# First layer of a two-layer hybrid mixer: norm scratch of the routings on other bytes, rotation and gate tables loaded with the mixer pools

## Chip, core and metric

The kernel runs on one core of a Trainium2 chip. Time is the device time of one execution in microseconds; three runs of the kernel before gave a median of 4283.43 us (4277.82 to 4283.72). TensorE is called PE here, VectorE DVE, ScalarE ACT, GpSimd POOL and SyncE SP; SP issues the plain loads, POOL the indirect ones.

## The reference, cut to what matters

Two layers work on 512 latent tokens x (four tiles of 128) and 256 context tokens (two tiles), 1024 wide. Each layer has a mixer of three parallel parts and then PEER, a retrieval from 16384 single-neuron experts. The context is needed through the first layer only. The function is this, with the arguments cut:

```python
for l in range(DEPTH):                       # 2
    hx = rmsnorm(x, norm1_g[l]) * (1.0 + sc1) + sh1
    hc = rmsnorm(ctx, norm1_g[l]) * (1.0 + csc1) + csh1
    yx, yc = token_mixer(hx, hc, ...)        # one input projection w_in; RG-LRU, latent attention, Hyena; w_out
    x = x + g1 * yx
    hx = rmsnorm(x, norm2_g[l]) * (1.0 + sc2) + sh2
    x = x + g2 * peer(hx, ...)
    if l < DEPTH - 1:                        # the same for ctx
        ctx = ctx + cg1 * yc ...; ctx = ctx + cg2 * peer(hc, ...)
return rmsnorm(x, final_g)

def block(xb):                               # peer, for 128 tokens
    q = (xb @ wq).reshape(T, 8, 256)         # 8 heads, two half queries against 128 keys each
    v1, i1 = lax.top_k(s1, 16); v2, i2 = lax.top_k(s2, 16)
    top_s, top_p = lax.top_k(cand, 16)       # 16 of the 256 sums
    eid, gate = ..., softmax(top_s)          # 128 experts for a token
    act = gelu(einsum('td,thkd->thk', xb, u_tab[eid]))
    return einsum('thk,thkd->td', gate * act, v_tab[eid])
```

## The kernel before

The program (`schedule`) writes down the first layer in this order: the context's mixer, with the Hyena filters and the modulation; the context's `route` (selection of experts, both tiles of kind "G"); x's mixer (`front`, `back`); the context's expert work; x's route and experts (`peer_x`); then the second layer. Experts are computed in one of two ways. For tiles of kind "D" (three of x's four in the first layer) `peer_x` multiplies with all experts: `ublock` makes 128 blocks of products (pst), `weights` builds the gates as one-hot products (og, o1, o2, pwt), `vblock` adds up the output (dacc). For tiles of kind "G" the rows of the chosen experts are gathered one row for each token at a time (`rows_of`, an indirect DMA on POOL into one of five buffers `grow`); DVE then does one step for each: `gtile_u` a product with a sum (acc and dot, L1100), `gtile_v` a weighted addition (acc, L1113). The context's two tiles and x's fourth are of kind G: 2 x 128 steps for each, 768 in the first layer.

Each piece of the program has a priority (`prio`): 1 for the context's mixer and its route, 3 for x, 6 for the gathers. A scheduler that builds the kernel sets each engine's order from the priorities and from its own estimate of when operands and bytes are ready; on the chip, each engine works its list in order. Tiles live in pools on a left and a right stack of on-chip memory; a tile of a later pool that lies on bytes of an earlier one has to wait until the last reader of the earlier one is done.

The steps that matter: `front` makes x's first norm (`transposed`: xr, xn, the transposes ptr, hT), loads w_in in 18 blocks (L522), multiplies (pwin, 16 matmul records for each block, 288 in all) and convolves (hc, xx, L545 and L547); then come the RG-LRU with its gate table gw (L704, read by L714) and Hyena (first spectral product ht, L651). `back` makes the latent attention `mla`, which loads the rotation tables ropep, ropec and ropes (L785 to L789; first read at L768), then the output projection pwo in four tiles, each followed by two DVE operations (wotmp, xs at L589 and L595), a store, and the second norm of that tile, which is the first step of x's `route`. `route` takes A2 and B2 (rows of the modulation), norms and transposes the tiles (into dhT for kind D, rhT for others), gives the norm's scratch back, and only then opens the pool rt with the keys, the weights wpq and the selections (top16: MAX8 at L981 and so on; experts: eid at L1060; gates). For the context both pools lie on the right stack at the same place, one after the other; for x the norm's scratch (`rn`) lies above what `back` has given back.

Of the kernel before, what the change touches and what calls it, by code (L numbers as in the profile page):

```python
# [71 lines left out]
class Kern:  # L72
# [50 lines left out]
    def run(self):  # L123
        tc, nc, a = self.tc, self.nc, self.a
        with ExitStack() as es:
# [16 lines left out]
            self.iota = pp.tile([128, 128], F32, name="iota")  # L142
            nc.gpsimd.iota(self.iota, pattern=[[1, 128]], base=0, channel_multiplier=0,
                           allow_small_or_imprecise_dtypes=True)
            self.iotah = pp.tile([128, 128], F16, name="iotah")
            nc.vector.tensor_copy(self.iotah, self.iota)
            self.ranks = pp.tile([128, 16, 8], F16, name="ranks")
            nc.vector.tensor_copy(self.ranks, self.iota[:, 0:16].unsqueeze(2).to_broadcast([128, 16, 8]))
# [24 lines left out]
    def schedule(self):  # L173
        a = self.a
        with ExitStack() as er:
# [31 lines left out]
            with self.prio(3):  # L207
                gx, ex = self.peer_x(0, 384, 6, 32, 32, (36, 46, 46), ex)
# [12 lines left out]
            with self.prio(5):  # L221
                gx, _ = self.peer_x(1, 320, 0, 32, 46, (44, 42, 42), ex)
# [231 lines left out]
    def front(self, es, ps, pr, l, s, low, side="left", split=True, ctx=False):  # L454
# [7 lines left out]
        st["cat"] = mp.tile([128, KD, L], F32, name="cat")  # L462
        st["cq"] = [mp.tile([128, L], F32, name=f"cq_{i}") for i in range(3)]
# [5 lines left out]
        st["u1"] = [lp.tile([128, L], F32, name=f"u1_{i}") for i in range(3)]  # L469
        sc = None  # L470
# [78 lines left out]
    def back(self, ps, pr, l, s, st, ex, mods=()):  # L549
# [6 lines left out]
        with self.pool(f"wo{l}{s}", side="right") as sp, ExitStack() as es2:  # L556
# [17 lines left out]
            tp = es2.enter_context(self.pool(f"wot{l}{s}", side=st["side"]))  # L574
            load(tp, later)
            g = self.load_row(tp, l, 0, s, "g1")
            for t in range(nt):
# [10 lines left out]
                tmp = tp.tile([128, D], F32, name="wotmp", bufs=2)  # L588
# [4 lines left out]
                else:  # L593
                    old = self.res[s][:, t, :]
                nc.vector.tensor_add(self.res[s][:, t, :], old, tmp)  # L595
                nc.sync.dma_start(self.sd[s][t], self.res[s][:, t, :])
                self.dump(f"xm{l}{s}{t}", self.res[s][:, t, :])
        self.src[s] = [self.sd[s][t] for t in range(nt)]

# [98 lines left out]
    def lru(self, ps, l, s, st, full, mp):  # L698
# [3 lines left out]
        with self.pool(f"lru{l}{s}", side="right") as sp:  # L702
            gw = sp.tile([128, 2, 2, 3, 128], F32, name="gw")
            nc.sync.dma_start(gw, a["lru_g"][l])  # L704
# [57 lines left out]

    def rope(self, sp, ps, t, rope):
# [10 lines left out]
    def mla(self, ps, pr, l, s, st, full, mods=iter(()), pool=None):  # L774
# [4 lines left out]
        with nullcontext(pool) if pool else self.pool(f"mla{l}{s}", side=st["side"]) as sp:  # L779
# [3 lines left out]
            if not s:  # L783
                pm = sp.tile([96, 96], F32, name="ropep")
                nc.sync.dma_start(pm, a["ropep"])  # L785
                cst = sp.tile([128, 512], F32, name="ropec")
                nc.sync.dma_start(cst[64:96, :], a["ropec"])
                snt = sp.tile([128, 512], F32, name="ropes")
                nc.sync.dma_start(snt[64:96, :], a["ropes"])  # L789
                rope = (pm, cst, snt)  # L790
# [99 lines left out]
    def route(self, ps, l, s, kinds, hT=None, iT=None, i2n=None, side="left", done=None, fill=iter(())):  # L890
# [8 lines left out]
        with ExitStack() as es:  # L899
            if hT is None:  # L900
# [16 lines left out]
            if done:  # L917
                done.close()
# [512 lines left out]
```

## Time and profile before

| | |
|---|---|
| median of 3 runs | 4283.43 us (4277.82 to 4283.72) |
| profiled execution | 4280.5 us |
| its span | 4278.7 us |
| mean granted clock of PE | 0.937 |
| PE busy | 3732.9 us, 87% |
| DVE busy | 3506.5 us, 82% |
| ACT, POOL busy | 44%, 36% |
| gathers' DMA queue | 604.05 MB, 40.6% of the 16 engines' span |
| chain that ended last | PE 33%, DMA 21%, DVE 17%, issue 16%, POOL 7% |

Busy time is an average over stages with different limits. In time the program runs like this: the context's mixer to about 371 us, the context's route to 538, x's projections to 609.5, Hyena and RG-LRU to about 690, latent attention to 829, output projection to 881, x's second norm and route to 1244, the dense experts to 2474, and the second layer from there to 4278.7. The chain of waits names, at each step, what released the next one; "issue" in it is time in which nothing that the profile shows was waited for.

### The profile page before, as it was taken

To read this page: it belongs to the slowest core of one execution; us is meant where nothing else is said; L and a number is where in the kernel's file an instruction comes from. 1 tells how busy PE (TensorE), PEld (TensorE's weight loads), DVE (VectorE), ACT (ScalarE), POOL (GpSimd) and SP (SyncE) were. 2 spreads that over 40 slices of the span, in tenths; PEclk is the share of its full clock that TensorE was granted. 3 is DMA by queue.
4 is the path that set the end of the run, shared out by engine and by line. 5 is a ranking of instruction groups with operands and counts; after the bars stand their busy time and mean duration, and the time that the engine had idled before them with its cause. 6 is when DMAs were issued, how large, how long until landed. Compare 5 with 4: busy or idle time off the path is not lost.

```text
span 4278.7 us, 63806 instructions
## 1 busy us (share of the span) xinstructions
PE 3732.9 (87%) x22530; PEld 2815.8 (66%) x22530; DVE 3506.5 (82%) x7435; ACT 1898.1 (44%) x3715; POOL 1524.6 (36%) x1225
## 2 busy tenths in 40 slices
PE   7887987968989989998868979887889999999997
PEld 3645544548878877877656657446888887776654
DVE  5746987889989988988898874754899998888988
ACT  4454342533247525622462233633325655555732
POOL 0000244652344563366426620000126345553243
PEclk7998997988999999999989989998999999999998
DMA  5554587885768897799879962252359888887697
GB/s 195 199 199 153 202 310 233 280 300 195 243 223 270 309 353 258 236 364 357 287 228 330 353 205 90 70 157 95 117 194 336 284 295 304 291 293 279 225 353 273
DMA packets 305154, 1062.90 MB, mean 248 GB/s; under 512 B 35468, under 2 KB 42336, under 8 KB 304834
## 3 DMA queue, kind: packets, MB, share of 16 engines
q0 software_dynamic: 165888, 604.05, 40.6%
q1 hardware_dynamic: 138946, 454.78, 30.5%
q8 instruction: 177, 2.90, 0.3%
q14 instruction: 143, 1.17, 0.1%
HBM read 1041.85 MB, written 16.84 MB: 247 GB/s over the span
## 4 chain that ended last, share of the span: by engine, by line
PE 33%; DMA 21%; DVE 17%; issue 16%; POOL 7%; ACT 5%; SPq 0%; POOLq 0%; DVEq 0%; ACTq 0%
PE pst L121 7%; POOL grow L1089 7%; DMA grow<-in_peer_u_dram,eid 6%; PE dacc L121 6%; DMA grow<-in_peer_v_dram,eid 5%; PE pwin L121 4%; DMA uv<-in_peer_ut_dram 4%; DMA uv<-in_peer_v_dram 4%; DVE uvl L114 3%; PE ppq L121 3%; DVE acc L1100 2%; DVE acc L1113 2%; DMA wmod<-in_w_mod_dram 2%; PE pwo L121 2%; PE fp L404 1%
## 5 line engine op out<-in xcount | busy, mean ns | idle before, releaser
L1089 POOL DMA_INDIRECT grow<-in_peer_u_dram,eid x576 | 754.0, 1309 | 1144.2 <-DVE acc L1100 562.0
L1089 POOL DMA_INDIRECT grow<-in_peer_v_dram,eid x576 | 762.7, 1324 | 767.3 <-DVE acc L1113 623.8
L121 PE MATMUL pst<-dhT,uvh 128*128 128x384 f32 (+1 forms) x4096 | 997.9, 328 | 0.0
L113 ACT CAST uvh<-uv 128x1024 fp32r<-128x1024 f32 x491 | 513.0, 1045 | 689.6 <-DMA uv<-in_peer_v_dram 414.2
L121 PE MATMUL pst<-dhT,uvl 128*128 128x384 f32 (+1 forms) x2048 | 695.1, 340 | 106.6 <-DVE uvl L114 75.0
L1113 DVE SCALAR_TENSOR_TENSOR acc<-grow,gate,acc 128x1024 f32<-128x1024 f32 x571 | 732.9, 1284 | 52.1 <-DMA grow<-in_peer_v_dram,eid 45.2
L1100 DVE SCALAR_TENSOR_TENSOR acc<-grow,ghx 128x1024 f32<-128x1024 f32 x576 | 704.6, 1223 | 66.7 <-DMA grow<-in_peer_u_dram,eid 61.3
L114 DVE TENSOR_TENSOR uvl<-uv,uvh 128x1024 fp32r<-128x1024 f32 x491 | 599.5, 1223 | 164.5 <-ACT uvh L113 160.5
L121 PEld LDWEIGHTS pst<-dhT,uvh 128*128 128x128 f32 x4096 | 729.8, 192 | 4.2 <-issue 2.2
L121 PEld LDWEIGHTS pst<-dhT,uvl 128*128 128x128 f32 x2048 | 394.3, 193 | 206.4 <-DVE uvl L114 154.8
L121 PE MATMUL dacc<-uvh,wl 128*128 128x512 f32 x1154 | 484.0, 420 | 38.5 <-DVE wl L114 22.3
L121 PE MATMUL dacc<-uvl,wh 128*128 128x512 f32 x1154 | 470.6, 408 | 20.4 <-DVE uvl L114 20.0
L121 PE MATMUL dacc<-uvh,wh 128*128 128x512 f32 x1154 | 466.3, 404 | 0.0
L1227 ACT ACTIVATE o<-iota,di2n 128x128 f16<-128x128 f32 x1056 | 325.5, 390 | 26.2 <-PE pwt L1231 26.0
L121 PEld LDWEIGHTS dacc<-uvh,wl 128*128 128x128 f32 x1154 | 222.3, 193 | 127.0 <-DVE wl L114 29.0
L121 PEld LDWEIGHTS dacc<-uvl,wh 128*128 128x128 f32 x1154 | 223.0, 193 | 79.2 <-DVE uvl L114 34.0
L121 PEld LDWEIGHTS dacc<-uvh,wh 128*128 128x128 f32 x1154 | 222.6, 193 | 48.8
L1231 PEld LDWEIGHTS <-o 128*128 128x128 f16 x4224 | 126.5, 97 | 113.3 <-DVE og L1217 33.4
L1231 PE MATMUL pwt<-og,o 128*128 128x46 f16 (+3 forms) x4224 | 152.5, 183 | 45.1 <-DVE og L1217 36.9
L1197 ACT ACTIVATE PA<-pst 128x384 f32<-128x384 f32 (+1 forms) x128 | 59.5, 464 | 281.7 <-PE pst L121 281.6
L1197 ACT ACTIVATE PB<-pst 128x384 f32<-128x384 f32 (+1 forms) x128 | 59.1, 462 | 222.7 <-PE pst L121 222.2
L254 POOL MEMSET rmod<- 128x512 f32 (+1 forms) x8 | 3.3, 416 | 422.8 <-DMA rows<-rmod 112.8
(398 smaller groups left out, 6122.2 us busy)
## 6 DMA issues: line engine op xcount, KB each, us to landing
uv<-in_peer_ut_dram SPq DMA_DIRECT2D x256, 512.0 KB
uv<-in_peer_v_dram SPq DMA_DIRECT2D x256, 512.0 KB
wmod<-in_w_mod_dram SPq DMA_DIRECT2D x96, 512.0 KB
wpq<-in_peer_wq_dram SPq DMA_DIRECT2D x48, 512.0 KB
w_in<-in_w_in_dram SPq DMA_DIRECT2D x72, 256.0 KB
w_in<-in_w_in_dram SPq DMA_DIRECT2D x18, 512.0 KB
grow<-in_peer_u_dram,eid POOLq DMA_INDIRECT x576, 6.5
grow<-in_peer_v_dram,eid POOLq DMA_INDIRECT x576, 6.7
```

The costliest lines, as they stand in the source:

```text
L113: self.nc.scalar.copy(hi, src)
L114: self.nc.vector.tensor_tensor(lo, src, hi.bitcast(F32), op=ALU.subtract)
L121: self.nc.tensor.matmul(p, w[i], x[j], start=start and n == 0, stop=stop and n == len(passes) - 1)
L254: nc.gpsimd.memset(r, 0.0)
L404: self.nc.tensor.matmul(p, w, x, start=(i == 0), stop=(i == len(pairs) - 1))
L1089: self.nc.gpsimd.indirect_dma_start(out=r, out_offset=None, in_=self.a[table], in_offset=bass.IndirectOffsetOnAxis(ap=eid[:, j:j + 1], axi ...
L1100: nc.vector.scalar_tensor_tensor(junk, r, 1.0, hx, op0=ALU.mult, op1=ALU.mult, accum_out=dot[:, j:j + 1])
L1113: nc.vector.scalar_tensor_tensor(acc, r, w[:, j:j + 1], acc, op0=ALU.mult, op1=ALU.add)
L1197: nc.scalar.activation(slot(i), p, AF.Gelu_apprx_tanh)
L1227: nc.scalar.activation(o2[:, q], self.iota, AF.Abs, bias=i2n[:, t, k * NC + q:k * NC + q + 1])
L1231: nc.tensor.matmul(p[:, q, :], o2[:, q, :], og[:, g, q, :], start=(g == 0), stop=(g == 1))
```

## The change

It has four parts, all in the first layer.

The context's route (`apart=True`) opens the pool rt first, then one for the norm (rn), then the one for rhT. The loads of wpq no longer lie on the norm's bytes.

x's route gets its norm's scratch from `back`: there a pool rn is opened beside the output projection's tiles, on bytes that the projection leaves free. The pool of the output weights stays open (`keep`) until the route's norm is done. To make room, the product of the gated residual is written into the result in place of wotmp, A2 and B2 lie in the last two rows of PA, the output norm's dhT is allocated behind PA, diT, di2n and one uvl, and PA has 31 slots and PB 33 instead of 32 and 32.

The table gw is allocated and loaded with the pool `lin` of the front, and the rope tables of x with the pool `mix`, both for the first layer only.

The 32-bit iota goes into a short-lived pool; only a 16-bit copy is kept, and ACT's form of o2 reads that.

```diff
 schedule:
-                gc = self.route(ps, 0, 1, "GG", side="right")
+                gc = self.route(ps, 0, 1, "GG", side="right", apart=True)
...
-                        ex = ExitStack()
-                        self.back(ps, pr, 0, 0, st, ex)
+                        ex, keep = ExitStack(), ExitStack()
+                        rn = self.back(ps, pr, 0, 0, st, ex, keep=keep)
+                        ex = (keep, ex)
...
-                gx, ex = self.peer_x(0, 384, 6, 32, 32, (36, 46, 46), ex)
+                gx, ex = self.peer_x(0, 384, 6, 31, 33, (36, 46, 46), ex, rn)
 front:
         st["cat"] = mp.tile([128, KD, L], F32, name="cat")
+        if l == 0 and not s:
+            st["rope"] = self.rope_tables(mp)
...
+        if l == 0:
+            st["gw"] = lp.tile([128, 2, 2, 3, 128], F32, name="gw")
+            nc.sync.dma_start(st["gw"], a["lru_g"][l])
 back:
-        with self.pool(f"wo{l}{s}", side="right") as sp, ExitStack() as es2:
+        rn = None
+        with ExitStack() as es1, ExitStack() as es2:
+            sp = (keep or es1).enter_context(self.pool(f"wo{l}{s}", side="right"))
...
+            if keep:
+                rn = keep.enter_context(self.pool(f"rn{l}{s}", side="right"))
...
-                tmp = tp.tile([128, D], F32, name="wotmp", bufs=2)
+                res = self.res[s][:, t, :]
+                tmp = res if l == 0 else tp.tile([128, D], F32, name="wotmp", bufs=2)
...
+        return rn
 route:
+            if apart:
+                rt = es.enter_context(self.pool(f"rt{l}{s}", side=side))
+                rn = es.enter_context(self.pool(f"rn{l}{s}", side=side))
...
-            with self.pool(f"rn{l}{s}", side=side) as sp:
-                A2 = self.load_row(sp, l, 2, s, "A2")
-                B2 = self.load_row(sp, l, 1, s, "B2")
+            with nullcontext(rn) if rn else self.pool(f"rn{l}{s}", side=side) as sp:
+                A2, B2 = rows or [sp.tile([128, D], F32, name=n) for n in ("A2", "B2")]
+                nc.sync.dma_start(A2, bcast_rows(self.rows[l, 2, s, :]))
+                nc.sync.dma_start(B2, bcast_rows(self.rows[l, 1, s, :]))
...
-            if done:
-                done.close()
-            sp = es.enter_context(self.pool(f"rt{l}{s}", side=side))
+            for stack in done:
+                stack.close()
+            sp = rt if apart else es.enter_context(self.pool(f"rt{l}{s}", side=side))
 peer_x:
-            hT = [dn.tile([128, KD, T], F32R, name=f"dhT{i}") for i in range(2)]
+            P = [dn.tile([128, nA, T], F32, name="PA")]
             iT = dn.tile([128, nt, 128 // NC, 4, NC, 2], F16, name="diT")
             i2n = dn.tile([128, nt, 128], F32, name="di2n")
+            low = [dn.tile([128, D], F32R, name="uvl", bufs=2)]
+            hT = [dn.tile([128, KD, T], F32R, name=f"dhT{i}") for i in range(2)]
...
-                lo = dn.tile([128, D], F32R, name="uvl", bufs=2)
+                lo = low.pop() if low else dn.tile([128, D], F32R, name="uvl", bufs=2)
```

The change also moves instructions in each engine's list, since the scheduler orders again with the new bytes. Lines of the kernel after are some 2 to 28 higher than those of the kernel before (L1126 and L1139 there are L1100 and L1113 here). Three places follow.

SP's list at the start of the context's route, before (wpq is a weight block of the route, xr, w_in and gw are x's mixer's):

```order
L921 DMA keysT<-in_peer_keys_dram 128x256
L294 DMA wpq<-in_peer_wq_dram 128x1024 x2
L424 DMA xr<-in_x_dram 128x1024 x2
L522 DMA w_in<-in_w_in_dram 128x1024
L294 DMA wpq<-in_peer_wq_dram 128x1024
L522 DMA w_in<-in_w_in_dram 128x1024
L294 DMA wpq<-in_peer_wq_dram 128x1024 x6
L522 DMA w_in<-in_w_in_dram 128x1024
L294 DMA wpq<-in_peer_wq_dram 128x1024
L522 DMA w_in<-in_w_in_dram 128x1024 x2
L294 DMA wpq<-in_peer_wq_dram 128x1024 x2
```

and after, from the rope tables on; keysT and two blocks of wpq stand ahead of them:

```order
L782 DMA ropep<-in_ropep_dram 96x96
L784 DMA ropec<-in_ropec_dram 32x512
L786 DMA ropes<-in_ropes_dram 32x512
L296 DMA wpq<-in_peer_wq_dram 128x1024 x14
L426 DMA xr<-in_x_dram 128x1024 x2
L529 DMA w_in<-in_w_in_dram 128x1024 x2
L426 DMA xr<-in_x_dram 128x1024
L476 DMA gw<-in_lru_g_dram 128x1536
L426 DMA xr<-in_x_dram 128x1024
L529 DMA w_in<-in_w_in_dram 128x1024 x15
L573 DMA wo_5247<-in_w_out_dram 128x1024
```

All blocks of the context's wpq now stand ahead of x's rows and of w_in; before, they alternated.

DVE's list around x's fourth Hyena convolution (hc) before; the lines between its parts are the route's weight splits (wpql), selections and gathers (L1100), of which eight stand ahead of row L545 of the next convolution:

```order
L545 TENSOR_SCALAR hc_4397<-upad,cols 128x512
L1100 SCALAR_TENSOR_TENSOR acc,dot<-grow,ghx 128x1024
L547 SCALAR_TENSOR_TENSOR hc_4397<-upad,cols,hc_4397 128x512
L114 TENSOR_TENSOR wpql<-wpq,wpqh 128x256
L547 SCALAR_TENSOR_TENSOR hc_4397<-upad,cols,hc_4397 128x512
L114 TENSOR_TENSOR wpql<-wpq,wpqh 128x256
L1100 SCALAR_TENSOR_TENSOR acc,dot<-grow,ghx 128x1024
L114 TENSOR_TENSOR wpql<-wpq,wpqh 128x256 x2
L1100 SCALAR_TENSOR_TENSOR acc,dot<-grow,ghx 128x1024 x2
L114 TENSOR_TENSOR wpql<-wpq,wpqh 128x256 x2
L1100 SCALAR_TENSOR_TENSOR acc,dot<-grow,ghx 128x1024
```

and after; here the route is over, and the gather steps between the convolutions are the 57th and those after it:

```order
L552 TENSOR_SCALAR hc_4407<-upad,cols 128x512
L1126 SCALAR_TENSOR_TENSOR acc,dot<-grow,ghx 128x1024
L554 SCALAR_TENSOR_TENSOR hc_4407<-upad,cols,hc_4407 128x512
L1126 SCALAR_TENSOR_TENSOR acc,dot<-grow,ghx 128x1024
L554 SCALAR_TENSOR_TENSOR hc_4407<-upad,cols,hc_4407 128x512
L1126 SCALAR_TENSOR_TENSOR acc,dot<-grow,ghx 128x1024 x3
L552 TENSOR_SCALAR hc_4408<-upad,cols 128x512
L1126 SCALAR_TENSOR_TENSOR acc,dot<-grow,ghx 128x1024
L554 SCALAR_TENSOR_TENSOR hc_4408<-upad,cols,hc_4408 128x512
L1126 SCALAR_TENSOR_TENSOR acc,dot<-grow,ghx 128x1024
L554 SCALAR_TENSOR_TENSOR hc_4408<-upad,cols,hc_4408 128x512
```

The convolutions stood inside the route, among its splits and selections; they stand behind the route now, between gather steps alone, some 50 gathers later.

DVE's list at the end of x's output projection, before: the last two of the four residual products (L589 on pwo, L595) and then the first tile's norm (nrm, nrt, nry, xn):

```order
L1113 SCALAR_TENSOR_TENSOR acc<-grow,gate,acc 128x1024 x8
L589 TENSOR_TENSOR wotmp<-pwo,g_6078 128x1024
L105 TENSOR_SCALAR nrm<-nss 128x1
L1113 SCALAR_TENSOR_TENSOR acc<-grow,gate,acc 128x1024
L595 TENSOR_TENSOR xs<-wotres,wotmp 128x1024
L106 RECIPROCAL nry<-nry 128x1
L105 TENSOR_SCALAR nrm<-nss 128x1
L106 RECIPROCAL nry<-nry 128x1
L107 SCALAR_TENSOR_TENSOR nrt<-nry,nrm 128x1 x2
L108 SCALAR_TENSOR_TENSOR nry<-nrt,nry 128x1
L1113 SCALAR_TENSOR_TENSOR acc<-grow,gate,acc 128x1024
L413 TENSOR_SCALAR xn<-xs,nry 128x1024
```

and after, the norm of the first tile (xn) ahead of the product of the second tile (L602 on pwo):

```order
L106 RECIPROCAL nry<-nry 128x1
L1139 SCALAR_TENSOR_TENSOR acc<-grow,gate,acc 128x1024
L107 SCALAR_TENSOR_TENSOR nrt<-nry,nrm 128x1
L1139 SCALAR_TENSOR_TENSOR acc<-grow,gate,acc 128x1024
L108 SCALAR_TENSOR_TENSOR nry<-nrt,nry 128x1
L1139 SCALAR_TENSOR_TENSOR acc<-grow,gate,acc 128x1024
L415 TENSOR_SCALAR xn<-xs,nry 128x1024
L1139 SCALAR_TENSOR_TENSOR acc<-grow,gate,acc 128x1024 x2
L602 TENSOR_TENSOR xs<-pwo,g_6083 128x1024
L1139 SCALAR_TENSOR_TENSOR acc<-grow,gate,acc 128x1024
L608 TENSOR_TENSOR xs<-wotres,xs 128x1024
```

The norms of the first two tiles moved in between the projection's products; those of the last two stay behind the last product.

## Rows read from the trace of the kernel before

**Rows 1.** Windows of the first layer: each engine's busy us, clock, DMA.
```profile
core 0: us, PE busy (x) PEld busy (x) DVE busy (x) ACT busy (x) POOL busy (x), PEclk, DMA share, GB/s
371.00:538.00 167.00, 145.90 (x853) 99.86 (x852) 142.50 (x614) 63.30 (x154) 28.86 (x38) 0.95 0.53 181
538.00:626.00 88.00, 79.47 (x190) 34.17 (x188) 79.78 (x146) 43.91 (x66) 49.41 (x37) 0.96 0.85 307
690.00:829.00 139.00, 121.26 (x614) 67.34 (x614) 118.80 (x216) 82.21 (x157) 82.97 (x67) 0.91 0.80 270
843.00:921.00 78.00, 44.56 (x118) 22.05 (x117) 63.10 (x74) 17.47 (x38) 44.19 (x36) 0.76 0.91 327
921.00:1244.00 323.00, 274.87 (x1849) 261.94 (x1849) 294.52 (x1091) 111.41 (x216) 104.27 (x85) 0.91 0.61 211
2240.00:2474.00 234.00, 211.62 (x774) 149.26 (x774) 193.49 (x180) 53.32 (x72) 143.69 (x108) 0.97 0.93 335
2474.00:2530.00 56.00, 25.30 (x94) 19.19 (x93) 51.56 (x80) 25.34 (x56) 20.16 (x22) 0.63 0.76 265
```

**Rows 2.** The page: VectorE's steps for gathered rows; their DMA queue.
```profile
L1113 DVE SCALAR_TENSOR_TENSOR acc<-grow,gate,acc 128x1024 f32<-128x1024 f32 x571 | 732.9, 1284 | 52.1 <-DMA grow<-in_peer_v_dram,eid 45.2
L1100 DVE SCALAR_TENSOR_TENSOR acc<-grow,ghx 128x1024 f32<-128x1024 f32 x576 | 704.6, 1223 | 66.7 <-DMA grow<-in_peer_u_dram,eid 61.3
q0 software_dynamic: 165888, 604.05, 40.6%
```

**Rows 3.** Windows of L1100, then L1113 alone: length, VectorE busy (instructions).
```profile
538.00:626.00 88.00, 44.38 (x74) 0.96 0.85 307
...
2474.00:2530.00 56.00, 24.88 (x20) 0.63 0.76 265
```

**Rows 4.** Timeline of PE: start, us, operation, [idle before, releaser].
```profile
207.03 4.44 PE L714 MATMUL lpg<-xx,gw 128*128 128x256 f32 x10 [8.33 <-DMA gw<-in_lru_g_dram]
...
694.96 1.99 PE L768 MATMUL bps<-kr,ropep 96*96 96x512 f32 x2 [11.06 <-DMA ropep<-in_ropep_dram]
...
902.63 1.94 PE L431 MATMUL ptr<-ident,xn 128*128 128x128 f32 x8 [21.86 <-DVE nry L108]
...
916.52 1.94 PE L431 MATMUL ptr<-ident,xn 128*128 128x128 f32 x8 [8.57 <-DVE nrt L107]
```

**Rows 5.** VectorE's groups, 371 to 538, x's convolutions: busy, mean ns.
```profile
L547 DVE SCALAR_TENSOR_TENSOR hc<-upad,cols,hc 128x512 f32<-128x512 f32 x12 | 9.0, 749 | 0.0
L547 DVE SCALAR_TENSOR_TENSOR xx<-upad,cols,xx 128x512 f32<-128x512 f32 x6 | 4.5, 748 | 0.0
L545 DVE TENSOR_SCALAR hc<-upad,cols 128x512 f32<-128x512 f32 x6 | 3.3, 545 | 0.9 <-ACT upad L501 0.9
```

**Rows 6.** Projection and hyena product of x: groups, timeline, tile, DMA issues.
```profile
L121 PE MATMUL pwin<-hT,w_in 128*128 128x512 f32 x167 | 78.6, 599 | 0.0
...
433.77 6.60 PE L121 MATMUL pwin<-hT,w_in 128*128 128x512 f32 x15
...
L121 PE MATMUL pwin<-hT,w_in x288: 591/592/1061, 415.2 to 609.5; 128*128 128x512 f32 x144
...
w_in<-in_w_in_dram SPq DMA_DIRECT2D x18, 512.0 KB
...
626.11 0.68 DVE L651 TENSOR_TENSOR ht<-hpf,hkk 128x512 f32<-128x512 f32 x1
```

**Rows 7.** Timeline of VectorE in the context's route: two selections, last eid.
```profile
466.69 0.89 DVE L981 MAX8 tv<-psc 128x8 f32<-128x128 f32 x4
...
513.11 0.89 DVE L981 MAX8 tv<-psc 128x8 f32<-128x128 f32 x4
...
537.94 0.22 DVE L1060 TENSOR_SCALAR eid<-pkb 128x64 int32<-128x64 f32 x1
```

**Rows 8.** PE's waits, 2180 to 2480: total us, times, longest.
```profile
PE pwt L1231 <- DVE og L1217: 28.6, 11, 2.9
PE dacc L121 <- DVE wl L114: 20.6, 12, 3.8
```

More of the change, by code (lines that the diff above doesn't have):

```diff
@@ L141, in run @@
             nc.scalar.activation(self.scc, self.scc, AF.Silu)
[L142 to L146, printed above, removed]
-            self.ranks = pp.tile([128, 16, 8], F16, name="ranks")
-            nc.vector.tensor_copy(self.ranks, self.iota[:, 0:16].unsqueeze(2).to_broadcast([128, 16, 8]))
+            self.iota = pp.tile([128, 128], F16, name="iota")
+            self.ranks = pp.tile([128, 16, 8], F16, name="ranks")
+            with self.pool("iota") as sp:
+                iota = sp.tile([128, 128], F32, name="iota32")
+                nc.gpsimd.iota(iota, pattern=[[1, 128]], base=0, channel_multiplier=0,
+                               allow_small_or_imprecise_dtypes=True)
+                nc.vector.tensor_copy(self.iota, iota)
+                nc.vector.tensor_copy(self.ranks, iota[:, 0:16].unsqueeze(2).to_broadcast([128, 16, 8]))
             self.scaled = {}
@@ L702, in lru @@
         with self.pool(f"lru{l}{s}", side="right") as sp:
-            gw = sp.tile([128, 2, 2, 3, 128], F32, name="gw")
-            nc.sync.dma_start(gw, a["lru_g"][l])
+            gw = st.get("gw")
+            if gw is None:
+                gw = sp.tile([128, 2, 2, 3, 128], F32, name="gw")
+                nc.sync.dma_start(gw, a["lru_g"][l])
             p4, n4, hb = self.decay(sp, l)
@@ L761, in rmsn, with rope_tables @@
             nc.vector.scalar_tensor_tensor(t, t, self.col(l, gname, i), rs, op0=ALU.mult, op1=ALU.mult)
+    def rope_tables(self, pool):
+        nc, a = self.nc, self.a
+        pm = pool.tile([96, 96], F32, name="ropep")
+        nc.sync.dma_start(pm, a["ropep"])
+        cst = pool.tile([128, 512], F32, name="ropec")
+        nc.sync.dma_start(cst[64:96, :], a["ropec"])
+        snt = pool.tile([128, 512], F32, name="ropes")
+        nc.sync.dma_start(snt[64:96, :], a["ropes"])
+        return pm, cst, snt
     def rope(self, sp, ps, t, rope):
@@ L783, in mla @@
             if not s:
[L784 to L790, printed above, removed]
+                rope = st.get("rope") or self.rope_tables(sp)
             if full:
@@ L887, in mla, with route @@
             values(*last)
-    def route(self, ps, l, s, kinds, hT=None, iT=None, i2n=None, side="left", done=None, fill=iter(())):
+    def route(self, ps, l, s, kinds, hT=None, iT=None, i2n=None, side="left", done=(), fill=iter(()), rn=None,
+              rows=None, apart=False):
         nc, a = self.nc, self.a
@@ L1147, in ended, with peer_x @@
         nc.sync.dma_start(self.out[t * 128:(t + 1) * 128, :][rows], res[rows])
-    def peer_x(self, l, T, vn, nA, nB, widths, ex):
+    def peer_x(self, l, T, vn, nA, nB, widths, done, rn=None):
         nc, a = self.nc, self.a
@@ L1258, in peer_x @@
             with self.banks(f"r{l}", "right", w=2, S=2) as ps:
-                gx = self.route(ps, l, 0, "D" * nd + "H" * (nt - nd) + "G" * (4 - nt), hT, iT, i2n, "right", ex, fill)
+                gx = self.route(ps, l, 0, "D" * nd + "H" * (nt - nd) + "G" * (4 - nt), hT, iT, i2n, "right", done, fill,
+                                rn, [free[:, (i - 2) * D:nA * T + (i - 1) * D] for i in range(2)] if rn else None)
             for _ in fill:
```

19 lines of the change are left out of this document (9 added, 10 removed).

## Prediction

> **What bounds the kernel now.** I read the busy shares first: TensorE (PE) is busy 87% of the span and VectorE (DVE) 82%, so neither bounds all of it, and a share says nothing of a stage. Then I read the first layer's stages one by one [rows 1] (layer 0 in the code). The reader should see four kinds. In the context's route with x's projections woven in (371 to 538) both engines are near full. From 538 on the expert gathers run beside everything: they are 1152 row gathers of 0.52 MB each (604 MB over 1152) [rows 2], and each one that lands needs a VectorE step of 1.22 or 1.28 us [rows 2]. Around the second norm (843 to 921) PE has 44.6 us of work in 78. In the tail of the expert product (2240 to 2474) PE has 211.6 of 234 and DVE 193.5. In the first norms of the next layer (2474 to 2530) PE idles and DVE is 92% full, and 20 of its steps there are gathers' [rows 3].
>
> I read the chain of waits next. From 538 to 626 it runs over the gathers (issue, landing, DVE step); so does the tail. The gathers are thus what fills DVE and DMA, and the question of this change is not how many there are (the same) but beside which stage they lie.
>
> Last I read PE's waits that the change aims at [rows 4]: 8.3 us for the gate table gw, 11.1 for the rotation table ropep, 21.9 for the first norm of the route of x (and 8.6 for a later tile, behind the 2.0 us of transposes that the first wait released).
>
> **What the order shows.** Two of the three moves do what they say: gw and the rope tables are issued earlier, and the norm of the first two tiles of x stands between the products of the output projection (third place in the order). The side effect is larger. The context's route now holds its own bytes to the end (rt beside rn beside rhT), and x's w_in buffers lie where rhT lies, so x's loads, transposes and projections all stand behind the context's route on SP, PE and DVE (first place). And since the gathers are the lowest priority and the route comes out first in the order, they move ahead of x's work: counted along DVE's order, the first hyena product of x (L651) comes after 56 gathers before and after 121 now; the output projection's first tile after 148 and 210; the first one-hot product of the dense part (og) after 267 and 339; the end of the dense product after 749 and 768, which is all of them.
>
> **The sum, part by part.** All of it against the profiled execution, 4280.5 us; its span is 4278.7.
>
> Tables and route: the gw wait is worth up to 8.3 us of the context's stage, where other filler work of PE may be what is late next; I take 6 (0 to 8.3). The context's route itself loses x's share: convolutions 9.0, 4.5 and 3.3 us of DVE [rows 5], with smaller ones about 20, and 167 of the 288 matmul records of pwin [rows 6], at the back-to-back pace of 6.60 us for 15 (0.44 each) 73 us of PE's 146. But what is left is a chain: its heads' selections start 15.5 us apart (three intervals from 466.7 to 513.1) and the last expert number comes 24.8 after the last of them, at 537.9 [rows 7]. In the order that chain keeps its own steps, has 24 gathers in it instead of 20 and one norm of x. I take 6 off for the freed engines, give 4 back for these five steps: its end goes from 538 to 538 - 6 - 6 + 4 = 530 us.
>
> Front of x: the first hyena product starts at 626.1 [rows 6]. From 530 on, three bounds.
> DVE: the 79.8 us that it has from 538 to 626, the 20 of x that came from the route, and 60 more gathers (121 less 24 is 97, against 37, which [rows 3] count twice for the read of their sums) at 1.25 are 75; with the 8 us that it idles there now 183, so 713, or 87 later.
> DMA: 97 gathers are 51 MB, 18 blocks of w_in [rows 6] 9.4, and x's rows, the output weights and the filters some 10 more: 70 MB. At the 335 GB/s of the tail [rows 1] 209 us; the blocks may start once the route's last scores are through, about 513, so 722, or 96 later. The Trainium skill, page "DMA: Bandwidth & Descriptors", section "Specifications", puts the HBM limit of a core at about 358 GB/s; by that the front would, as an estimate, be 83 later; no stage of [rows 1] is above it.
> PE: the fourth norm of x stands ten gathers behind the route in DVE's order, so pwin starts near 543; 288 matmuls take 127 at 0.44, and 170 at the pace that they have from 538 to 609.5 beside gathers (121 in 71.5, 0.59 each; first and last in [rows 6]); then 16.6 to the hyena product as now. 687 or 730, 61 or 104 later.
> I take 95 later, near the middle of the three, with ends 61 (PE alone at its best) and 109 (DVE's 175 us of work at the 85% that it reaches in 690 to 829 [rows 1], from 530 on).
>
> Latent attention: the rope wait of 11.1 is gone, and 89 gathers instead of 92 stand up to the projection, 3 x 1.28: 15 less (5 to 18; 5 if DVE, 85% busy there, is the next one late).
>
> Projection, norm and route of x: PE's 21.9 and 8.6 can go, since the norms of tiles 0 and 1 lie beside pwo. But who ends last there is DVE: 63.1 us in 78, the rest waits for gathers to land at 327 GB/s. Its work is the same, 129 gathers up to the first og instead of 119 are 13 us more, in a route that has it 91% busy. The freed norm brings 14 or so. I take 1 less, with ends 30 less (PE's view) and 17 more.
>
> Dense part: the order is the same, with 353 gathers instead of 357 in it: 5 less (0 to 8).
>
> Tail: from the 132nd og to the end 76 gathers instead of 125. That is 49 x 1.28 = 63 us of DVE, but PE has 211.6 of 234 there, so no more than 22 can come off, and a little of the 28.6 and 20.6 us in which PE waits for og and wl around its start [rows 8]. I take 15 less (2 to 30).
>
> Next layer's first norms: 19 gathers fewer, 24 us of DVE; what stays is a chain over ACT, DVE and PE for each tile. 12 less (5 to 25).
>
> Sum: 95 - 15 - 1 - 5 - 15 - 12 = 47 later. 4280.5 + 47 = 4327.5; the median of the runs shown lies 2.9 above the profiled execution, so 4330. The ends, all added, are 50 earlier and 114 later. The reason in one line: some 70 gathers leave stages in which PE or a chain is the next bound, and go to one in which DVE and DMA are already full.
>
> **Rivals.**
> *Faster.* The late stages pay in full. The tail's chain of waits runs over gathers, which speaks for it; PE's 90% speaks against. If the front costs only PE's 61, and the later stages give back 15 + 30 + 5 + 25 + 20 = 95, the time is 34 less, 4250. It turns on the later stages giving more than 70 while the front stays at PE's bound; that needs DVE to find 75 us in a stage where it idles 8.
> *No change.* Front at 75, since the gathers' waits there shrink with more of them ready, and the later stages give 75 (15 + 15 + 5 + 25 + 15): about 4283. This is also where it ends if the weave of x into the route was worth little.
> *Slower than forecast.* Without pwin PE has 73 us of work in a route of 160, under half. The granted clock was 0.63 in 2474 to 2530, where PE worked 25.3 of 56 us, and 0.76 in 843 to 921, with 44.6 of 78, against 0.95 in the route now [rows 1]. At 0.63 the 73 us become 110; the scores wait for these products, so most of the 37 us lies on the path: 4367. The Trainium skill, page "TensorE: Matmul & The Clock Gate", Part 1, says that the half rate is the array's default and that activity releases it; by that rule the emptied route falls back to 1.2 GHz between its bursts and the 37 us are due; the trace agrees in the two emptiest stages.
> *It doesn't do what it says.* The norms stay late, because DVE reaches them late behind its gathers: that is in the term of 1 above and alone costs 14 more, within the forecast's range.
>
> **How the numbers follow.** Forecast 0.57, with its own range 4298 to 4362; slower than forecast 0.20; faster 0.13; no change 0.10. A measurement of this kernel can tell about 0.2% (9 us) from no change. The range that leaves out some 2 in 10 is 4276 to 4380. Faster by over 0.2%: 0.13; within: 0.10; slower: 0.77.
>
> **What would show it.** The route's last expert number at 527 to 535; pwin then in one piece, from about 543 to 690 or later; the first hyena product at 715 to 735; no wait for ropep or gw; PE's gap after pwo under 8 us; some 340 gathers done at the first og; no gather after the dense product's end, where 20 are now. Wrong it is if the first hyena product comes before 690 (DVE was not full, gathers hide), or if the tail from the 132nd og on shrinks by over 30 us (the gathers, not PE, set it).

## The result

The changed kernel takes 4385.14 us (median of four runs, 4371.15 to 4395.55) against 4283.58 before; the ratio is 1.0236, 95% interval 1.0213 to 1.0259. The direction was forecast, the size was not: 47 later forecast, 101.6 measured, just beyond the range's end of 4380. In the profiled executions the span grows from 4278.7 to 4384.2 us.

The stages of the changed kernel that answer to [rows 1], in the same columns (window and length, busy us of each engine with instructions, granted clock, share of the DMA engines, GB/s):

```profile
357.00:524.00 167.00, 95.65 (x689) 84.82 (x688) 126.45 (x576) 52.63 (x126) 36.74 (x33) 0.76 0.45 161
524.00:737.00 213.00, 163.29 (x380) 73.48 (x380) 173.10 (x310) 62.97 (x103) 119.72 (x111) 0.86 0.88 318
936.00:1013.00 77.00, 46.22 (x123) 22.28 (x122) 61.67 (x77) 21.41 (x47) 44.00 (x33) 0.78 0.89 320
1013.00:1356.00 343.00, 282.98 (x1844) 270.19 (x1845) 306.00 (x1171) 107.10 (x207) 121.08 (x98) 0.88 0.62 215
2357.00:2576.00 219.00, 204.76 (x768) 146.79 (x767) 134.50 (x133) 53.60 (x72) 72.17 (x57) 0.97 0.67 239
2576.00:2612.00 36.00, 19.65 (x72) 14.52 (x72) 23.67 (x52) 24.38 (x55) 0.00 (x0) 0.67 0.26 87
```

The first two are to be read against 371 to 538 and 538 to 626. The context's route is as long as before though it has lost x's work: PE works 95.7 us in it instead of 145.9. The projections of x behind it take 213 us instead of 88, and no engine is full in them: DVE works 173 of 213, PE 163, the DMA engines 0.88. What DVE does in the rest is in its waits in that stage (for whom, total us, times, longest), first changed and then before, in the 88 us:

```profile
DVE acc L1126 <- DMA grow<-in_peer_u_dram,eid: 37.3, 36, 2.9
```

```profile
DVE acc L1100 <- DMA grow<-in_peer_u_dram,eid: 7.8, 7, 1.7
```

The norm stage (936 to 1013) is as long as before, the route of x (1013 to 1356) 20 us longer than in [rows 1], and the tail (2357 to 2576) has PE as its bound, as its 204.8 of 219 us show.

One table holds the stages of the kernels run, but for three experiments on the front stage that are told with it. Each entry is the difference between the starts of two named instructions in the kernel's own trace: the context route's last expert number (eid) at DVE; the first hyena product of x (ht); the first residual product behind the output projection; the first dense product (pst); the first one-hot product (og); the first read of the dense product's sum (dacc); the next layer's first convolution; the end.

| kernel | eid at | to ht | to projection | to pst | to og | to dacc | to next conv. | to end |
|---|---|---|---|---|---|---|---|---|
| before | 537.9 | 88.2 | 216.6 | 78.1 | 323.1 | 1230.6 | 47.4 | 1756.8 |
| changed | 524.5 | 212.3 | 199.2 | 77.0 | 343.0 | 1219.8 | 36.0 | 1772.4 |
| changed, second time | 537.1 | 215.5 | 200.1 | 77.0 | 347.0 | 1207.6 | 36.6 | 1764.6 |
| together | 547.3 | 90.3 | 202.6 | 77.3 | 329.6 | 1224.8 | 46.8 | 1767.9 |
| apart alone | 533.1 | 210.7 | 205.2 | 79.7 | 337.3 | 1214.3 | 37.1 | 1766.1 |
| tables alone | 550.8 | 89.5 | 202.6 | 76.6 | 319.4 | 1227.9 | 47.5 | 1759.8 |
| norm alone | 540.9 | 90.1 | 209.6 | 77.3 | 331.8 | 1234.5 | 47.7 | 1765.7 |
| rhT on the left | 548.0 | 89.0 | 202.7 | 75.7 | 333.4 | 1231.7 | 47.4 | 1767.3 |
| rope alone | 541.1 | 93.0 | 198.9 | 78.7 | 322.3 | 1227.0 | 47.6 | 1763.5 |
| rope and wkvb | 544.5 | 94.1 | 183.0 | 81.0 | 320.0 | 1231.9 | 46.8 | 1766.1 |

Two of its columns say how far a single execution can be trusted: the second layer, the same instructions in all, is 1757 to 1772 long, and the context's mixer ahead of the first column ends early or some 10 us later (the second norm of its second tile starts at 330 to 337 us or at 344 to 345), the changed kernel once each. So a single entry in those two is no sign of the change. The late starts are not spread evenly, though: of the profiles with the gate table loaded early (the table's five and the three experiments told apart from it) seven start that norm at 339 us or later and one at 332.0, while all five without it start at 330 to 337. So the early gate table may cost the context's mixer some 10 us; no run separates it from the spread. In all kernels that have only a part of the change, the short-lived iota, the residual product in place and the new order of tiles in `peer_x` stay, whatever their name says. The medians below are each taken against runs of the kernel before on the same chip, whose own medians were 4281.94 to 4290.66.

### The profile page after: what moved, and what is told of

The parts are those of the page before. It is cut to its first block, busy times and chain, and to the rows that moved or that the text cites. A ratio compares the mean times of both kernels' runs of the same rounds, so it can differ in the third digit from the quotient of the medians.

```text
span 4384.2 us, 63784 instructions
## 1 busy us (share of the span) xinstructions
PE 3759.8 (86%) x22530; PEld 2838.7 (65%) x22530; DVE 3511.7 (80%) x7435; ACT 1903.2 (43%) x3719; POOL 1531.7 (35%) x1225
## 4 chain that ended last, share of the span: by engine, by line
PE 34%; DMA 21%; DVE 18%; issue 15%; POOL 6%; ACT 5%; SPq 0%; POOLq 0%; DVEq 0%; ACTq 0%
PE dacc L121 8%; PE pst L121 7%; DMA grow<-in_peer_u_dram,eid 6%; POOL grow L1115 6%; DMA grow<-in_peer_v_dram,eid 5%; DMA uv<-in_peer_ut_dram 4%; PE pwin L121 4%; DMA uv<-in_peer_v_dram 3%; DVE uvl L114 3%; DVE acc L1139 2%; DVE acc L1126 2%; PE ppq L121 2%; ACT uvh L113 1%; PE pwo L121 1%; PE pwt L1259 1%
## 5 line engine op out<-in xcount | busy, mean ns | idle before, releaser
L1115 POOL DMA_INDIRECT grow<-in_peer_u_dram,eid x576 | 744.5, 1292 | 1356.2 <-DVE acc L1126 570.4
L1115 POOL DMA_INDIRECT grow<-in_peer_v_dram,eid x576 | 779.2, 1353 | 728.4 <-DVE acc L1139 529.5
L1126 DVE SCALAR_TENSOR_TENSOR acc<-grow,ghx 128x1024 f32<-128x1024 f32 x576 | 704.1, 1222 | 90.5 <-DMA grow<-in_peer_u_dram,eid 84.6
L1139 DVE SCALAR_TENSOR_TENSOR acc<-grow,gate,acc 128x1024 f32<-128x1024 f32 x571 | 732.1, 1282 | 45.2 <-DMA grow<-in_peer_v_dram,eid 38.6
L1255 ACT ACTIVATE o<-iota,di2n 128x128 f16<-128x128 f16 x1056 | 325.2, 390 | 31.1 <-PE pwt L1259 30.9
L1225 ACT ACTIVATE PA<-pst 128x320 f32<-128x320 f32 (+1 forms) x126 | 58.4, 463 | 310.8 <-PE pst L121 308.5
L1259 PE MATMUL pwt<-og,o 128*128 128x46 f16 (+3 forms) x4224 | 152.6, 183 | 41.0 <-DVE og L1245 32.7
```

Source lines behind the costliest of these rows:

```text
L1115: self.nc.gpsimd.indirect_dma_start(out=r, out_offset=None, in_=self.a[table], in_offset=bass.IndirectOffsetOnAxis(ap=eid[:, j:j + 1], axi ...
L1126: nc.vector.scalar_tensor_tensor(junk, r, 1.0, hx, op0=ALU.mult, op1=ALU.mult, accum_out=dot[:, j:j + 1])
L1139: nc.vector.scalar_tensor_tensor(acc, r, w[:, j:j + 1], acc, op0=ALU.mult, op1=ALU.add)
L1225: nc.scalar.activation(slot(i), p, AF.Gelu_apprx_tanh)
L1255: nc.scalar.activation(o2[:, q], self.iota, AF.Abs, bias=i2n[:, t, k * NC + q:k * NC + q + 1])
L1259: nc.tensor.matmul(p[:, q, :], o2[:, q, :], og[:, g, q, :], start=(g == 0), stop=(g == 1))
```

## The experiments

**Which part costs the time.** The changed kernel with the old route of the context:

```diff
-                gc = self.route(ps, 0, 1, "GG", side="right", apart=True)
+                gc = self.route(ps, 0, 1, "GG", side="right")
```

> The changed kernel with the context's route as it was (rt after the norm's pool, so the weave of x's loads and projections into the route comes back; along VectorE's order 56 gathers stand ahead of the first hyena product again, not 121); early tables and the norm's scratch in the projection stay. Theory A, the context's route alone costs the time: first hyena product 4 to 8 us earlier than in the kernel before (626), total 4260 to 4275. Rival B, the loss sits in several parts (the norm's bytes, the new place of dhT, the uv buffers): total 4300 or more, with the route and norms of x from the output projection to the first og longer than the 401 us of before by 15 or more.

Measured 4290.28 us, ratio 1.0015 (0.9997 to 1.0034). The loss is gone, but so is the gain that theory A gave the other parts: the total and the first hyena product (637.6 us) are later than theory A had them, and from the output projection to the first og it takes 406.9 us, less than rival B asked. The other way round, the kernel before with the separate pools of the context's route alone (and the 16-bit iota):

```diff
+            if apart:
+                rt = es.enter_context(self.pool(f"rt{l}{s}", side=side))
+                rn = es.enter_context(self.pool(f"rn{l}{s}", side=side))
```

> The kernel before with only the context's route changed (rt opened first, apart) and the short-lived 32-bit iota. Theory A: the whole loss is here, first hyena product at 735 to 745, and without the tables' gain the total is 4385 to 4405. Rival B: the loss is shared among the parts, total 4310 to 4350.

Measured 4379.11 us, ratio 1.0227 (1.0175 to 1.0279): all of the loss, in the same stage (210.7 us from eid to ht; first hyena product at 743.8 us, as theory A has it, the total 6 us below its range).

**What the other parts bring.** The early loads alone:

```diff
+            st["rope"] = self.rope_tables(mp)
...
+            st["gw"] = lp.tile([128, 2, 2, 3, 128], F32, name="gw")
+            nc.sync.dma_start(st["gw"], a["lru_g"][l])
```

> The kernel before with only the early loads of the gate and rotation tables. Theory A: the two waits of 8.3 and 11.1 us on PE go and nothing of the same size takes their place: total 4264 to 4272 (12 to 19 less). Rival C, the waits covered others that are now late: total 4278 to 4284, and PE waits for other operands at the same two places for 5 us or more.

Measured 4282.30 us, ratio 1.0002 (0.9983 to 1.0021): rival C by its total. The two waits are gone. At the first place the gate's products start at 192.8 us instead of 207.0, yet the context's mixer ends no earlier; at the second PE waits for the next operand. In the kernel with the tables alone, PE's waits from 640 to 720 us:

```profile
PE bps L822 <- DMA wkvb<-in_mla_wkvb_dram: 10.4, 1, 10.4
```

That is 10.4 us for wkvb where [rows 4] had 11.1 for ropep. And the norm's scratch in the output projection, alone (with PA's 31 slots and the new order of tiles):

```diff
-                        self.back(ps, pr, 0, 0, st, ex)
+                        rn = self.back(ps, pr, 0, 0, st, ex, keep=keep)
+                        ex = (keep, ex)
```

> The kernel before with only the norm's scratch of x's route in the output projection (and the new order of tiles in the expert product). Theory A, VectorE and the gathers' landings end last there: the wait of 21.9 us before the first transposes shrinks, others come between the norms, and the first og comes between 5 us earlier and 5 us later, total 4276 to 4290. Rival D, PE's gap was what counted: first og 20 to 30 us earlier, total 4253 to 4265.

Measured 4288.64 us, ratio 1.0009 (0.9989 to 1.0029): theory A by its total, with the first og 5.9 us later, just past its 5. The first dense product stands where it stood (77.3 us behind the projection's first tile, 78.1 before), because PE's one wait of 21.9 us in [rows 4] became several. Timeline of PE in this kernel (start, us, operation, idle before it and what ended that):

```profile
896.73 1.11 PE L433 MATMUL ptr<-ident,xn 128*128 128x128 f32 x4 [16.81 <-DVE hraw L446]
...
904.22 1.94 PE L433 MATMUL ptr<-ident,xn 128*128 128x128 f32 x8 [4.86 <-ACT dhT L113]
912.23 1.12 PE L433 MATMUL ptr<-ident,xn 128*128 128x128 f32 x4 [6.08 <-DVE hraw L446]
...
918.00 0.66 PE L121 MATMUL pst<-dhT,uvl 128*128 128x384 f32 x1 [2.43 <-DVE uvl L114]
```

The transposes of the first tile (878.88, ahead of these lines), of the second (896.73) and of the third (904.22) are early: the third's start 63.5 us behind the first residual product, where it was 73.8 before. But pst does not come sooner: ACT's copies of the third tile stand in its list behind the split of the first expert block (uvh), and that waits for the block's load. ACT's wait from 890 to 919 us:

```profile
ACT uvh L113 <- DMA uv<-in_peer_ut_dram: 5.5, 1, 5.5
```

The copies, the transposes of the fourth tile and pst follow behind it. After that the route of x has five more gathers in it (90 instead of 85 from pst to og) and is 8.7 us longer.

**What sets the 212 us.** Rows' landings or DVE's steps? The changed kernel with half-width steps, transfers unchanged:

```diff
+            w = slice(0, 512 if l == 0 else D)
-            nc.vector.scalar_tensor_tensor(junk, r, 1.0, hx, ...)
+            nc.vector.scalar_tensor_tensor(junk[:, w], r[:, w], 1.0, hx[:, w], ...)
```

> The changed kernel with VectorE's step for a gathered row of table u in the first layer on 512 of its 1024 columns (the other half of that sum is left out); the transfers are the same. In the order 129 gathers stand ahead of the first hyena product, not 121. The stage from the route's last expert number to that product took 212 us in the changed kernel, VectorE waited 37 us in it for rows to land. Theory L, the landings of rows set this stage: 200 to 225. Rival V, VectorE's steps set it: about 100 steps are 0.6 shorter, so 145 to 165.

From eid to ht 203.0 us: theory L. The whole kernel took 4380.99 us in its one run. The mirror image, half the bytes and whole steps:

```diff
-    def rows_of(self, table, eid, j):
+    def rows_of(self, table, eid, j, w=D):
...
-        self.nc.gpsimd.indirect_dma_start(out=r, out_offset=None, in_=self.a[table],
+        self.nc.gpsimd.indirect_dma_start(out=r[:, :w], out_offset=None, in_=self.a[table].rearrange("n (a b) -> (n a) b", b=w),
...
+            if l == 0:
+                r = self.rows_of("peer_u", eid, j, 512)[:, :512].unsqueeze(1).to_broadcast([128, 2, 512])
...
```

> The changed kernel with gathers of half the bytes from table u in the first layer (512 columns of other rows, which VectorE reads twice, so its steps are as long as before). 125 gathers stand ahead of the first hyena product. Theory L, landings set the stage of 212 us: without 25 MB of its 68 VectorE is next with 173 us of work, so 175 to 190. Rival V, VectorE's steps set it: 205 to 215. If neither counts but the number of buffers and the latency of one gather: 200 to 212, with waits for landings left.

188.7 us, in the range of theory L. The whole kernel took 4318.32 us in its one run, where the route of x (332.5) and the dense part (1181.7) are shorter too. The windows of that stage, first with half steps, then with half rows, and DVE's wait for landings in each:

```profile
532.00:735.00 203.00, 162.90 (x378) 73.00 (x377) 125.67 (x312) 65.44 (x105) 103.52 (x115) 0.88 0.92 343
```

```profile
DVE acc L1127 <- DMA grow<-in_peer_u_dram,eid: 69.0, 57, 4.7
```

```profile
535.00:724.00 189.00, 157.88 (x380) 72.28 (x380) 175.10 (x316) 63.86 (x103) 127.65 (x114) 0.90 0.70 231
```

```profile
DVE acc L1127 <- DMA grow<-in_peer_u_dram,eid: 10.7, 8, 3.2
```

With half steps DVE has 47 us less to do and waits 32 us more: the DMA engines are at 0.92 and 343 GB/s. With half rows they are at 0.70 and DVE is full, 175 of 189. So the transfers are the larger bound in the changed kernel, and DVE's work stands 24 us behind as the next one. They are not the only one: with half steps three more gathers went through the stage (99 steps instead of 96 by the traces) in 9 us less, so the rate of 318 GB/s is no fixed limit there. A gather can only start when a buffer is free, and POOL waits in this stage of the changed kernel for DVE's step on the buffer:

```profile
POOL grow L1115 <- DVE acc L1126: 42.2, 30, 6.0
```

The third experiment asks whether it is the rate or the turn of a buffer:

```diff
-        r = self.gp.tile([128, D], F32, name="grow", bufs=5)
+        r = self.gp.tile([128, D], F32, name="grow", bufs=4)
...
-        row = dict(name="grow", bufs=5)
+        row = dict(name="grow", bufs=4)
```

> The changed kernel with four buffers for gathered rows instead of five. 97 gathers in 212 us on five buffers are 10.9 us for each turn of a buffer. Theory L as a rate of the DMA engines (318 GB/s in this stage): 207 to 222 from the route's last expert number to the first hyena product. Rival B, the turn of a buffer sets it: 94 x 10.9 / 4 is 256, so 240 to 260.

From eid to ht 220.9 us, the upper end of the rate's range and far from the buffers' 256, at 302 GB/s and with two gather steps fewer in the stage. The whole kernel took 4505.80 us in its one run: the front is 4% longer, and the stages with gathers behind it 4 to 7% (the route of x 360.8 us instead of 343.0). So the fifth buffer is worth something everywhere, and no more in the front than elsewhere.

**Separate pools, or the bytes under rhT?** The changed kernel with rhT of the context's route on the left stack:

```diff
-                hp = es.enter_context(self.pool(f"rh{l}{s}", side=side))
+                hp = es.enter_context(self.pool(f"rh{l}{s}", side="left" if apart else side))
```

> The changed kernel with one tile pool moved: rhT of the context's route lies on the left stack, where x's mixer tiles come later, and no longer on the bytes of x's w_in. All else of the change stays, the separate pools of the route too. In the order, x's loads and projections stand inside the route again and 56 gathers ahead of the first hyena product. Theory M, the loss came from rhT lying on w_in's bytes and not from the separate pools: first hyena product at 620 to 640, total 4275 to 4295. Rival S, the separate pools themselves cost time on the chip: total over 4330.

Measured 4293.24 us, ratio 1.0007 (0.9996 to 1.0018), first hyena product at 637.0 us, 89.0 us behind eid: theory M. The pools of the route are still apart; only x's w_in no longer lies on rhT, and x's work is back inside the route: SP issues the first blocks of w_in from 378.6 us on. In the changed kernel they start at 498.9, when the route's last product from rhT (ppq) is through. SP's wait there, from 470 to 560 us:

```profile
SPq L529 <- PE ppq L121: 15.8, 1, 15.8
```

**A version that is faster.** The wait that moved from ropep to wkvb asked for one more load. First the rotation tables without the gate table:

> The kernel before with the early load of the rotation tables alone; the gate table stays where it was. If the wait of 11.1 us was worth its length: total 4269 to 4276. Rival C, the next load on SP's list, wkvb, is late at the same place (10.4 us were measured when both tables came early): no change, 4280 to 4287, with a wait for wkvb of 8 us or more.

Measured 4275.76 us, ratio 0.9987 (0.9971 to 1.0003), with PE waiting 9.5 us for wkvb: rival C by its wait, while the time lies in the range of the first expectation, and the interval holds 1. Then with wkvb as well:

```diff
+            st["rope"] = self.rope_tables(mp)
+            st["wkvb"] = mp.tile([128, 2, 768], F32, name="wkvb")
+            nc.sync.dma_start(st["wkvb"], a["mla_wkvb"][l])
```

> The kernel before with the rotation tables and also wkvb loaded with x's mixer pool. With the rotation tables alone PE waited 9.5 us for wkvb at the same place. If that was only one wait in place of another: 8 to 11 us less than with the tables alone in the stage up to the output projection, total 4262 to 4272. If a third operand is late there (wqb, or VectorE): total 4272 to 4282.

Measured 4266.59 us, ratio 0.9940 (0.9924 to 0.9957): faster than both kernels, by 0.6% against the kernel before, with an interval clear of 1. The stage from ht to the projection is 183.0 us instead of 198.9, and the window of it shows PE nearer to full than the 171.0 of 199 that it had with the rotation tables alone:

```profile
639.00:822.00 183.00, 167.30 (x784) 98.35 (x785) 162.75 (x305) 82.34 (x163) 99.72 (x81) 0.94 0.77 262
```

Of the 16 us some are not the wait's: eight gathers fewer stand in the stage (81 against 89 steps by the traces), some 10 us of DVE, and nine are done behind the next layer's first convolution, where none was with the rotation tables alone. How the 16 divide was not run.

**Once more.** The changed kernel again, for the second layer's 15 us:

> The changed kernel once more. Its second layer took 1772 us from the first convolution of x there to the end, against 1757 in the kernel before, with the same instructions; in the other kernels run it was 1760 to 1768. If the 15 us belong to the change: 1768 to 1776 again. If it is a spread between executions: anything from 1757 to 1772; the first layer's part stays within 3 us of 2612.

Measured 4391.26 us, ratio 1.0238 (1.0212 to 1.0264) in its own runs. The second layer took 1764.6 us this time and the first layer's part ended at 2620.8, 9 later and not within the 3 expected: both are spread between executions, and the table's front stage (215.5), route (347.0) and tail come again.

## Why the prediction was right or wrong

In the profiled execution the span grew by 58.5 us more than forecast. The front of x has 15.7 of them, projection, norm and route of x 19.8, dense part and tail 9.2, the next norms 0.6 and the second layer 15.6; latent attention gave 2.4 more than forecast. The first two are the steps that failed; the entries of the dense part and of the second layer did not come again in that size in the second execution.

*That the route's bytes move x's work and the gathers, and that this costs more than the rest gains*: right, and shown three ways (undone, alone, and by moving rhT). The separate pools are harmless; rhT on w_in's bytes is the cause.

*The context's tables and route*: the forecast took 8 us off, to 530. The gate wait went and the route ended at 524.5 once and 537.1 the second time. The route itself is 144.6 to 146 us from its first selection to its last eid in three profiles with separate pools and 145.4 before. So against the kernel before x's share of PE and DVE in it was free, and the 6 us given to freed engines were not there. Against the changed kernel with rhT on the left, which has the weave and all the rest of the change, they were: its route takes 151.0. With the weave the route is 145.4 and 145.7 (norm alone) or, in the five kernels with early rotation tables, 148.1 to 152.6; why, stays open.

*The front of x*: forecast 95 later, measured 110.7 (ends 61 to 109). From eid the forecast's own duration was 191 us, and 212 came. Of the three bounds the one that binds most is DMA, and it was mis-sized: 67.8 MB moved in the window where 70 were estimated, but at 318 GB/s, not the 335 of the tail (213 us instead of 202), and the blocks of w_in could not start at 513. SP issued two of them at 498.9, and the other sixteen only as w_in's two buffers came free, from 553.9 on, since pwin started at 544.2 (543 forecast) behind x's norms. Until then few loads ran beside the gathers: 296 GB/s from 524 to 554. There is a second loss that the forecast's three separate bounds could not hold: DVE's list is worked in order, so a step of x waits behind gathers that have not landed. Timeline of DVE in the changed kernel around Hyena's first step hab, and of PE at the same time:

```profile
715.29 1.23 DVE L1126 SCALAR_TENSOR_TENSOR acc<-grow,ghx 128x1024 f32<-128x1024 f32 x1 [1.32 <-DMA grow<-in_peer_u_dram,eid]
...
717.86 1.22 DVE L1126 SCALAR_TENSOR_TENSOR acc<-grow,ghx 128x1024 f32<-128x1024 f32 x1 [1.33 <-DMA grow<-in_peer_u_dram,eid]
...
720.36 1.23 DVE L1126 SCALAR_TENSOR_TENSOR acc<-grow,ghx 128x1024 f32<-128x1024 f32 x1 [1.27 <-DMA grow<-in_peer_u_dram,eid]
...
721.51 0.42 DVE L640 TENSOR_TENSOR hab<-hc 128x255 f32<-128x255 f32 x1
```

```profile
722.07 0.45 PE L650 MATMUL hptr<-ident,hab 128*128 128x128 f32 x1 [13.67 <-DVE hab L640]
```

Of the twelve gather steps from 694 us to hab ten wait 1.3 us for their row. PE's last product of pwin ends at 704.2, and from 708.4 on PE idles 13.7 us for a DVE step of 0.4; the 16.6 us that the forecast put from pwin to the hyena product became 32.5.

*Latent attention*: forecast 15 less, measured 17.4 less. The size was right and the reason only in part: the wait for ropep was replaced by one of 10.4 us for wkvb, which the forecast should have named, since wkvb stands in the same pool, one place ahead of ropep on SP's list, and that pool opens only when Hyena's bytes come free (with the rotation tables alone, SP waits 15.2 us at wkvb for the DVE step that writes Hyena's output; in the kernel before it issues wkvb at 686.6 us and ropep at 687.0). With the separate pools alone and no tables early the stage is 205.2, 11.4 less than before, and with the norm alone, whose list is the same up to there, 209.6; so 216.6 in the profile before is itself on the long side. How the 17 divide stays open.

*Projection, norm and route of x*: forecast 1 less, measured 19 more, past the upper end of 17. The step that failed is "the freed norm brings 14 or so". From the first residual product to pst it brought 1 (77.0 us instead of 78.1). The norms did come sooner: the transposes of the third tile start 61.8 us behind that product instead of 73.8:

```profile
997.76 1.94 PE L433 MATMUL ptr<-ident,xn 128*128 128x128 f32 x8 [4.85 <-ACT dhT L113]
```

But the first dense product needs the first expert block too, and SP issues its load behind the store of the last residual tile (992.0 us in the changed kernel). ACT's wait for it, from 985 to 1014 us:

```profile
ACT uvh L113 <- DMA uv<-in_peer_ut_dram: 7.0, 1, 7.0
```

Behind this wait stand ACT's copies of the third tile, the transposes of the fourth and pst. In the kernel before ACT has no such wait. How much of the 12 us an earlier load of this block would free was not run. PE's gap behind the projection, forecast under 8 us, was 14.4 and then 4.9 and 7.6. The other half, more gathers in the route, was sized well: 99 from pst to og instead of 85, and 19.9 us, 1.4 each. Over the kernels the stage follows that count: 85 gathers 323.1 us, 90 (norm alone) 331.8, 94 (apart alone) 337.3, 99 (changed) 343.0.

*Dense part and tail*: forecast 20 less together, measured 10.8 less at the first time and 23.0 at the second. The tail's 15 came as 16.1 and 18, and the reason holds: with its gathers gone (77 gather steps from the 132nd og on, where 125 were) DVE is down to 134.5 of 219 us and PE, at 204.8, keeps the stage. *Next layer's first norms*: 12 forecast, 11.4 measured.

*The rival that the clock falls*: the granted clock in the emptied route did fall, to 0.76 from 0.95, as the Trainium skill, page "TensorE: Matmul & The Clock Gate", Part 1, has it for an array that idles. But no loss shows: the route is as long as before, where the rival had most of 37 us on its path. The 0.76 is a mean over the clock's two levels in a stage where PE works 95.7 of 167 us. Whether the lower clock took back what the freed engines gave is not shown.

*The rival that it gets faster* named its own point: the later stages had to give more than 70. From the hyena product to the next layer's first convolution they gave 20.8 (110.7 less 89.9, by the starts in the two traces).

*Second layer*: forecast 0; it is 15.6 us longer in the profile and 7.8 at the second time, within the spread of the table. By the sums of the profiled execution, 110.7 - 17.4 - 1.1 + 19.9 - 10.8 - 11.4 + 15.6 = 105.5, the growth of the span.

## What to carry to other kernels

When tile pools move, look first at which later tile lands on the bytes of which earlier one, and at what the order then does: here one pool's place turned two interleaved stages into one behind the other, and a filler of low priority slid into the stage that could hide it least. A wait for a load is worth its length only if the next operand is there: see when the load's bytes come free and where it stands on its issuer's list, and move the loads that start at that moment together. Here ropep gave way to wkvb, and the early norm to the load of the first expert block. And of several bounds on a stage none may be taken alone where engines work lists in order: a step behind a late transfer waits for it, whatever that step costs.

## What the runs showed of the hardware

The transfers of the changed front stage ran at 318 GB/s over 213 us, and the rate was not constant: in 40 slices of 5.3 us they moved from 52 to 415 GB/s, the highest from 684 us on, where the last block of w_in, the output weights and then the tables of Hyena were loaded beside the gathers. The row of the DMA view from 524 to 737, GB/s of each slice:

```profile
GB/s 243 364 244 308 317 321 361 283 342 356 299 303 322 395 233 306 311 308 196 325 280 280 314 256 352 352 323 138 312 349 402 415 409 408 406 409 412 413 315 52
```

The Trainium skill, page "DMA: Bandwidth & Descriptors", section "Specifications", puts the HBM limit at about 358 GB/s; these slices are above it, and the prediction's remark that no stage is above it holds for whole stages only. The kernel before has such slices too, up to 418 GB/s between 538 and 626. And with one buffer for gathered rows fewer, four instead of five, the changed kernel took 121 us longer in its one run (4505.80 against 4385.14).
